# One gate vector of the second layer moves from a row sum to the array, together with changes to banks and instruction order

## The chip, the core and the metric

The kernel runs on one core of a Trainium2 chip. The metric is the device time of one execution in microseconds (us). A core has TensorE (PE), VectorE (DVE), ScalarE (ACT), GpSimd (POOL, unused here) and SyncE (SP), whose queue issues nearly all DMA transfers of this kernel, in program order.

## The reference, cut to what matters

A two-layer transformer step on 384 tokens (one context block of 128 tokens, two latent blocks of 128), 1,024 wide, all in 32-bit floats:

```
mod = silu(cond) @ w_mod[l] + b_mod[l]
sh1, sc1, g1, sh2, sc2, g2 = jnp.split(mod[:, None, :], 6, axis=-1)
u = layer_norm(x) * (1.0 + sc1) + sh1
h = mixer_ab(u, ...) if l == 0 else mixer_cd(u, ...)
x = layer_norm(ALPHA * x + g1 * h, ln_g[l, 0], ln_b[l, 0])
u = layer_norm(x) * (1.0 + sc2) + sh2
x = layer_norm(ALPHA * x + g2 * swiglu(u, w_gate[l], w_up[l], w_down[l]), ln_g[l, 1], ln_b[l, 1])
...
def swiglu(u, w_gate, w_up, w_down):
    return (jax.nn.silu(u @ w_gate) * (u @ w_up)) @ w_down
```

Each layer needs six vectors `mod` of 1,024 numbers, for two conditions (context, latent). Vector (l, v) is the v-th of layer l; (1, 2) is the gate `g1` of layer 1, which is first needed after the second mixer.

## The kernel before, in words

The program goes through layer 0 (mixer AB, output projection, FFN) and layer 1 (mixer CD, output projection, FFN). A 32-bit product is made in three passes (`PASSES`): both operands are split into a rounded part (`r_`, ACT cast, L173) and a rest (`l_`, DVE subtract, L175), and r·r, r·rest and rest·r are summed in PSUM. Weights arrive as pieces of 512 KB in a ring of five buffers `raw` (`raw_unit`), all on SP's queue.

*Modulation vectors* are made in two ways. `mod_pe` multiplies the raw pieces (`rawm`, in the `raw` ring) on the array: 8 pieces, 4 matmuls of 32x256 each. `mod_steps` loads them as `mraw` into the four buffers of the pool `s`, two of which hold the sums `z`. For each of 8 pieces it adds piece times condition to `z` on DVE (L249; the first piece is a multiply on ACT, L246). Then it sums over partitions with 8 matmuls by ones (L254, tile `mod`), scales (`bm`, L258 to L261) and, except for gates, turns the row into columns (`mod_cols`, tile `modc`). A gate's row goes to DRAM (`gs`, 8 small DMAs) and is read back later.

`SMODS` lists the vectors that the two FFNs make with `mod_steps`: six in FFN 0, one in FFN 1. `TMODS` lists those made with `mod_pe` in the transition between the layers, none before. `steps` is called twice for each of ten column groups of an FFN. Before, a call takes up to `MSTEP` pieces, and after a vector's last piece one call is left out.

*Output projection and heads* (`w_out_phase`). For each token block b: projection and residual (`P`), two LayerNorms, then `F` = `to_u`: 8 transposes into two PSUM banks (`puo_b_0`, `puo_b_1`), scaled by ACT or DVE into `ufo`, cast to `urf`, with rest `ulf`. Then `H` = `head`: the first 256 columns of gate and up projection (`hg`, `hu`), their SwiGLU product `hsg`, two transposes (`ht`), and the split `hhr`, `hhl`. `bankTO` hands out two banks, T and O, in turn; `puo` and `ht` share them. The string `WORDER` gives the program order; a scheduler may reorder within an engine, and `boost` raises an operation's priority.

*FFN* (`ffn_phase`): `wg` and `wu` products of 128x384 (L542, two banks of `bankA`), SwiGLU on ACT and DVE (`sg`, `hr`, `hl`), and `dn`, which accumulates the down projection in six banks.

*Transition*: `DORDER` interleaves the last down projections of layer 0 (`D`), LayerNorm (`A`, `B`), transposes (`F`, tiles `pud`, `ufd`, `ur`, `ul`) with `T` = `tail_block`, the first block of the second mixer's slab 1 (`cd_0`). In it `keep_busy` issues `NBUSY` matmuls of 128x512 whose result nobody reads (`idle_d`, L129). `M` = `tail_mod` is defined but not in `DORDER`. After it slab 1 goes on with blocks 1 and 2 (`cd_1`, `cd_2`), then slab 0, 2, 4 and 3. `tck` are transposes of the cached keys `ck`, `tcd` those of a slab's result.

```
for _ in range(MSTEP):
    if next(gen, False):
        st["pause"] = 1
        return
```

Of the kernel before, what the change touches and what calls it, by code (L numbers as in the profile page):

```python
# [19 lines left out]
P = 128  # L20
# [3 lines left out]
NTOK = NB * P  # L24
# [2 lines left out]
HOLD = 4  # L27
RHOLD = (3, 5)
WMODS = ((), ())
TMODS = ()  # L30
SMODS = (((0, 5), (1, 1), (1, 0), (1, 3), (1, 4), (1, 2)), ((1, 5),))
NLNW = 8
AORDER = "Q0 R0 W4 T G0 D V0 M0 Q1 W12 M1 G1 C0 E M2 N1 R1 N2 V1 C1 X N0 N4 N3 N5"
NIDLE = (5, 4)
NFILL = 2
NBUSY = 12
LOADS = (("m", 0, 1), ("kv", 0), ("m", 1, 1), ("q", 0), ("m", 2, 2), ("q", 2), ("m", 4, 2), ("kv", 4), ("q", 4), ("m", 6, 2), ("q", 6))
WORDER = ("P0 P1 G A0 B0 F0 A1 B1 P2 U H0 F1 A2 B2 F2 X H1 M H2", "G P0 P1 A0 B0 A1 B1 U P2 F0 F1 H0 A2 B2 F2 X H1 M H2")
CORDER = "V0 V1 N0 V2 C N1 N2"
DORDER = "D0 A0 D1 B0 A1 F0 U B1 D2 T A2 F1 B2 F2 K"  # L40
NWR = 5
NHEAD = 2
MSTEP = 4
KORDER = ((2, 3, 0, 1), (3, 0, 1, 2))
WDEPTH = 2
RGB = 1
# [18 lines left out]
def trunk_kernel(ctx: ExitStack, tc: tile.TileContext, a: dict):  # L65
    nc = tc.nc
    mm = nc.tensor.matmul
# [169 lines left out]
    def mod_steps(l, v, out):  # L237
        w = a["w_mod"][l].rearrange("(p k) n -> p k n", k=KC)
        bm = mod_tile(l, v)
        z = [big([P, D], f"z{l}_{v}_{c}") for c in range(2)]  # L240
        for k in range(KC):
            t = big([P, D], f"mraw{l}_{v}_{k}")
            SY.dma_start(t, w[:, k, v * D : (v + 1) * D])
            for c in range(2):
                if k == 0:
                    S.mul(z[c], t, cs[:, c, k : k + 1])  # L246
                else:
                    with gated():
# [12 lines left out]
        V.scalar_tensor_tensor(bm, ps[:, 256:512], selc[:, 1:2], bm, ALU.mult, ALU.add)  # L261
        out.append((bm, ps))
# [171 lines left out]
    def w_out_phase(l, pre, cat, x, gt, lnv, u2, sh2, sc2, wx, hh, bankTO, mods):  # L434
# [26 lines left out]
            next(st[b][1])  # L461

        def to_u(b):
            last[b] = make_u(b, st[b][0], sh2, sc2, u2, f"o{l}_{b}", bankTO, b == 2)

        def mod_all():
            for ll, v in mods:
# [2 lines left out]
        def hold_splits():  # L470
            gate[0] = last[2]

        def head(b):
            ps = bankA(f"hg{l}_{b}")
            in_block(ps, u2, units2["g"], b, 256)
            sg = mid([P, 256], f"hsg{l}_{b}")
            S.activation(sg, ps[:, 0:256], AF.Silu)
            ps = bankA(f"hu{l}_{b}")
            in_block(ps, u2, units2["u"], b, 256)
            V.tensor_tensor(sg, ps[:, 0:256], sg, ALU.mult)  # L480
            pt = bankTO(f"ht{l}_{b}")
            for q in range(NHEAD):
                boost(nc.tensor.transpose, pt[:, q * P : (q + 1) * P], sg[:, q * P : (q + 1) * P], ident)
            cat_split(hh, 0, NHEAD, slice(b * P, (b + 1) * P), pt[:, 0 : NHEAD * P])

        run_order(WORDER[l], {"P": project, "A": norm, "B": norm, "F": to_u, "H": head,
                              "G": lambda: head_units("g", a["w_gate"]), "U": lambda: head_units("u", a["w_up"]),
                              "M": mod_all, "X": hold_splits})
        bk.close()


    NF = D_FF // P

    def ffn_phase(l, u2, x, lnp, hh, wx_es, pto, get_g, lnv, steps, keep, late, tail_units, tail_block, tail_mod):
        wg = a["w_gate"][l].rearrange("(k p) f -> p k f", p=P)
        wu = a["w_up"][l].rearrange("(k p) f -> p k f", p=P)
        wd = a["w_down"][l]
# [3 lines left out]
        def load_down(fc, rl=None):  # L501
            return split_unit(wd[fc * P : (fc + 1) * P, :], [D], f"wd{l}_{fc}", rl)

        wx_es.close()
        pto.close()
        fes = ExitStack()
        fpool = fes.enter_context(pool(f"ffn{l}"))
        accp = Banks(f"pd{l}", D=6)
        for fc in range(NHEAD):
# [24 lines left out]
        def proj(w, fp, nm):
            un = [split_unit(w[:, 4 * i : 4 * i + 4, fp * 256 : (fp + 1) * 256], [4, 256], f"{nm}{l}_{fp}_{i}")
                  for i in range(2)]
            ps = [bankA(f"{nm}{l}_{fp}_{j}") for j in range(2)]
            for i in range(2):
                for j in range(2):
                    for k in range(4):  # L540
                        for pu, pw in PASSES:
                            mm(ps[j][:, 0:NTOK], un[i][pw][:, k, j * P : (j + 1) * P], u2[pu][:, 4 * i + k, :],  # L542
                               start=(i == 0 and k == 0 and pu + pw == 0),
                               stop=(i == 1 and k == 3 and pw == 1))
            return ps

        for fp in range(NHEAD // 2, NFP):
            pg = proj(wg, fp, "wg")
            sg = []
            for j in range(2):  # L550
                t = fpool.tile([P, NTOK], F32, tag="sg", name=f"sg{l}_{fp}_{j}", bufs=2)
# [790 lines left out]
    m = {}  # L1342
    xscr = dram.tile([NB, P, D], F32, tag="xscr", name="xscr")
    for l in range(2):
# [31 lines left out]
        u2 = new_u(f"f{l}")  # L1376
        wx, wx_es = opened(f"wx{l}")
        hh = tuple(lnp.tile([P, NHEAD, NTOK], F32R, name=f"hh{q}{l}") for q in "rl")
        w_out_phase(l, pre, cat, x, gt, lnv, u2, m[l, 3], m[l, 4], wx, hh, bankTO, WMODS[l])
        if wxr_es is not None:  # L1380
            wxr_es.close()
        cat_es.close()
# [48 lines left out]
        def steps(fp, i):  # L1431
            if fp == NFP:
                for _ in gen:
                    pass
                at_end()
                return
            if st["pause"]:
                st["pause"] -= 1
                return
            for _ in range(MSTEP):  # L1440
                if next(gen, False):
                    st["pause"] = 1
# [78 lines left out]
```

## Time and profile before

| | |
|---|---|
| Median of three runs | 1017.21 us (1017.24, 1013.7, 1017.21) |
| The profiled execution's own time | 1012.87 us |
| Its span in the trace | 1011.1 us |
| PE busy | 984.2 us, 97% |
| DVE busy | 668.2 us, 66% |
| ACT busy | 436.5 us, 43% |
| DMA read | 167.52 MB, 170 GB/s over the span |

All times in the trace are those of the profiled execution, from the start of its span. Its own time is 1.8 us above the span and 4.3 us below the median. PE's matmuls overlap in the records: an instruction's duration is longer than the distance to the next start, and the distance of starts tells what it costs.

### The profile page before, as it was taken

The numbers are of one execution on the slowest core, as the hardware profiler recorded it, in microseconds if no ns is written. First come the engines' busy times: TensorE is split into PE (matmuls) and PEld (weight loads), VectorE is DVE, ScalarE is ACT, GpSimd is POOL, SyncE is SP. The second block draws the span as 40 slices with busy tenths as digits, with TensorE's granted clock in tenths as the row PEclk, the third lists the DMA queues.
The fourth block names the chain that finished last, engine by engine and source line by source line (L and its number), as shares of the span: only waits on it lengthen the run. The fifth ranks groups of instructions, "written<-read, shape, count | busy, mean of one in ns | idle before, by whom it ended". The sixth has DMA issues, their size and how long they took to land.

```text
span 1011.1 us, 14717 instructions
## 1 busy us (share of the span) xinstructions
PE 984.2 (97%) x5583; PEld 824.0 (81%) x5583; DVE 668.2 (66%) x1368; ACT 436.5 (43%) x790; POOL 1.2 (0%) x5
## 2 busy tenths in 40 slices
PE   9999999999999999999999999999899999999996
PEld 4775567787999888988987766787799999999985
DVE  5387558588875777968978577558895333335554
ACT  3395533228533333334427556544943333333410
POOL 0000000000000000000000000000000000000000
PEclk9999999999999999999999999999999999999999
DMA  9975446473674867768744332235575444444401
GB/s 306 296 205 189 147 140 206 167 252 102 211 229 149 279 203 252 210 219 258 231 168 151 99 95 94 84 106 222 156 237 169 160 123 126 125 124 125 156 22 42
DMA packets 109704, 172.85 MB, mean 171 GB/s; under 512 B 10177, under 2 KB 78273, under 8 KB 109633
## 3 DMA queue, kind: packets, MB, share of 16 engines
q1 hardware_dynamic: 106960, 170.87, 53.0%
q10 hardware_dynamic: 2672, 1.04, 0.4%
q8 instruction: 44, 0.72, 0.3%
q14 instruction: 28, 0.22, 0.1%
HBM read 167.52 MB, written 4.36 MB: 170 GB/s over the span
## 4 chain that ended last, share of the span: by engine, by line
PE 81%; DVE 8%; DMA 4%; ACT 4%; issue 2%; ACTq 0%; DVEq 0%
PE dn L518 17%; PE wg L542 15%; PE wu L542 15%; PE cd L377 7%; PE wo L377 4%; PE rvg L377 3%; PE s L377 3%; DMA rawm<-in_w_mod 2%; PE rqk L377 2%; PE mod L118 2%; DVE z L249 1%; PE ms L118 1%; PE hg L377 1%; PE wpo L118 1%; PE idle L129 1%
## 5 line engine op out<-in xcount | busy, mean ns | idle before, releaser
L249 DVE SCALAR_TENSOR_TENSOR z<-mraw,cs,z 128x1024 f32<-128x1024 f32 x98 | 121.0, 1281 | 12.0 <-DMA mraw<-in_w_mod 11.5
L542 PE MATMUL wg<-urf,r_wg 128*128 128x384 f32 x320 | 108.5, 340 | 3.1 <-DVE sg L559 1.7
L542 PE MATMUL wg<-ulf,r_wg 128*128 128x384 f32 x320 | 108.4, 339 | 0.0
L542 PE MATMUL wu<-ulf,r_wu 128*128 128x384 f32 x320 | 108.2, 338 | 0.0
L542 PE MATMUL wu<-urf,r_wu 128*128 128x384 f32 x320 | 108.2, 340 | 0.0
L542 PE MATMUL wg<-urf,l_wg 128*128 128x384 f32 x320 | 108.1, 338 | 0.0
L542 PE MATMUL wu<-urf,l_wu 128*128 128x384 f32 x320 | 108.1, 338 | 0.0
L175 DVE TENSOR_TENSOR l_wg<-raw_wg,r_wg 128x1024 fp32r<-128x1024 f32 x40 | 48.6, 1224 | 56.2 <-ACT r_wg L173 56.2
L173 ACT CAST r_wd<-raw_wd 128x1024 fp32r<-128x1024 f32 x36 | 37.8, 1049 | 92.0 <-PE wu L542 47.6
L175 DVE TENSOR_TENSOR l_wd<-raw_wd,r_wd 128x1024 fp32r<-128x1024 f32 x36 | 44.0, 1223 | 48.4 <-ACT r_wd L173 48.4
L173 ACT CAST r_wg<-raw_wg 128x1024 fp32r<-128x1024 f32 x40 | 42.0, 1051 | 69.2 <-PE dn L518 32.6
L175 DVE TENSOR_TENSOR l_wu<-raw_wu,r_wu 128x1024 fp32r<-128x1024 f32 x40 | 48.7, 1223 | 33.6 <-ACT r_wu L173 33.6
L518 PE MATMUL dn<-l_wd,hr 128*128 128x512 f32 x168 | 66.6, 396 | 0.0
L518 PE MATMUL dn<-r_wd,hr 128*128 128x512 f32 x168 | 66.6, 396 | 0.0
L518 PE MATMUL dn<-r_wd,hl 128*128 128x512 f32 x168 | 66.5, 396 | 0.0
L542 PEld LDWEIGHTS wg<-urf,r_wg 128*128 128x128 f32 x320 | 60.1, 188 | 6.3 <-DVE sg L559 2.5
L173 ACT CAST r_wu<-raw_wu 128x1024 fp32r<-128x1024 f32 x40 | 42.0, 1049 | 52.9 <-issue 24.7
L542 PEld LDWEIGHTS wu<-urf,r_wu 128*128 128x128 f32 x320 | 60.1, 188 | 2.2 <-ACT r_wg L173 0.8
L542 PEld LDWEIGHTS wu<-ulf,r_wu 128*128 128x128 f32 x320 | 60.1, 188 | 0.5
L542 PEld LDWEIGHTS wg<-ulf,r_wg 128*128 128x128 f32 x320 | 60.1, 188 | 0.4
L542 PEld LDWEIGHTS wg<-urf,l_wg 128*128 128x128 f32 x320 | 60.1, 188 | 0.0
L542 PEld LDWEIGHTS wu<-urf,l_wu 128*128 128x128 f32 x320 | 60.1, 188 | 0.0
(415 smaller groups left out, 2164.2 us busy)
## 6 DMA issues: line engine op xcount, KB each, us to landing
mraw<-in_w_mod SPq DMA_DIRECT2D x56, 512.0 KB
raw_wd<-in_w_down SPq DMA_DIRECT2D x44, 512.0 KB
raw_wg<-in_w_gate SPq DMA_DIRECT2D x40, 512.0 KB
raw_wu<-in_w_up SPq DMA_DIRECT2D x40, 512.0 KB
rawm<-in_w_mod SPq DMA_DIRECT2D x24, 512.0 KB
raw_cd<-in_w_in_cd SPq DMA_DIRECT2D x20, 512.0 KB
ms<-in_w_mod SPq DMA_DIRECT2D x16, 512.0 KB
raw_rqk<-in_w_in_ab SPq DMA_DIRECT2D x16, 256.0 KB
```

The costliest lines, as they stand in the source:

```text
L118: return f(*args, **kw)
L129: mm(ps[0 : lhs.shape[-1], 0 : rhs.shape[-1]], lhs, rhs, start=True, stop=True)
L173: S.copy(r, t)
L175: V.tensor_tensor(lo, t, r, ALU.subtract)
L249: V.scalar_tensor_tensor(z[c], t, cs[:, c, k : k + 1], z[c], ALU.mult, ALU.add)
L377: op = mm(ps[:, col : col + width], u[pu][:, k0 + kk, b * P : (b + 1) * P], (r, lo)[pw][:, kk, :], start=(first and i == 0 and pu + pw == ...
L518: mm(acc[b, nh], h[fc][ph][:, b * P : (b + 1) * P], wrl[pw][:, nh * 512 : (nh + 1) * 512], start=(fc == 0 and ph + pw == 0), stop=(last an ...
L542: mm(ps[j][:, 0:NTOK], un[i][pw][:, k, j * P : (j + 1) * P], u2[pu][:, 4 * i + k, :], start=(i == 0 and k == 0 and pu + pw == 0), stop=(i ...
```

## The change

Vector (1, 2) leaves `SMODS` and enters `TMODS`; `DORDER` runs `M0` right after `T`. The twelve `idle_d` matmuls go (`NBUSY = 0`). `steps` takes two pieces in every call, without a pause: 20 calls of two are the 40 pieces of the five vectors that are left in FFN 0. In `w_out_phase`, `to_u` takes the projection's banks W and V for blocks 1 and 2 and no longer T and O, and the end of a head (`head_end`: `ht`, `hhr`, `hhl`) is written after the next head's gate block, the last one after the FFN's first `wg` projection. The first multiply of a vector is put under `gated()`.

```diff
-TMODS = ()
-SMODS = (((0, 5), (1, 1), (1, 0), (1, 3), (1, 4), (1, 2)), ((1, 5),))
+TMODS = ((1, 2),)
+SMODS = (((0, 5), (1, 1), (1, 0), (1, 3), (1, 4)), ((1, 5),))
-NBUSY = 12
+NBUSY = 0
-DORDER = "D0 A0 D1 B0 A1 F0 U B1 D2 T A2 F1 B2 F2 K"
+DORDER = "D0 A0 D1 B0 A1 F0 U B1 D2 T M0 A2 F1 B2 F2 K"
-MSTEP = 4
+MSTEPS = (2, 2)
...
                 if k == 0:
-                    S.mul(z[c], t, cs[:, c, k : k + 1])
+                    with gated():
+                        S.mul(z[c], t, cs[:, c, k : k + 1])
...
         def to_u(b):
-            last[b] = make_u(b, st[b][0], sh2, sc2, u2, f"o{l}_{b}", bankTO, b == 2)
+            tags = iter((None, "WV", "WW")[b] or ())
+            bank = bankTO if b == 0 else lambda nm: bk(next(tags), nm)
+            last[b] = make_u(b, st[b][0], sh2, sc2, u2, f"o{l}_{b}", bank, b == 2)
...
+        heads = []
+
         def head(b):
             ps = bankA(f"hg{l}_{b}")
             in_block(ps, u2, units2["g"], b, 256)
+            if heads:
+                head_end(*heads.pop())
...
             V.tensor_tensor(sg, ps[:, 0:256], sg, ALU.mult)
+            heads.append((b, sg))
+
+        def head_end(b, sg):
             pt = bankTO(f"ht{l}_{b}")
             for q in range(NHEAD):
-                boost(nc.tensor.transpose, pt[:, q * P : (q + 1) * P], sg[:, q * P : (q + 1) * P], ident)
+                nc.tensor.transpose(pt[:, q * P : (q + 1) * P], sg[:, q * P : (q + 1) * P], ident)
             cat_split(hh, 0, NHEAD, slice(b * P, (b + 1) * P), pt[:, 0 : NHEAD * P])
...
+        return lambda: head_end(*heads.pop())
...
+        first = proj(wg, NHEAD // 2, "wg")
+        end_heads()
+        wx_es.close()
+        pto.close()
...
-            pg = proj(wg, fp, "wg")
+            pg = first if fp == NHEAD // 2 else proj(wg, fp, "wg")
...
-            if st["pause"]:
-                st["pause"] -= 1
-                return
-            for _ in range(MSTEP):
-                if next(gen, False):
-                    st["pause"] = 1
-                    return
-
-        st = {"pause": 0}
+            for _ in range(MSTEPS[i]):
+                next(gen, None)
```

Three places where instructions move. The first is PE in the transition, from the end of slab 1's block 0 (`cd_0`) on. Before:

```order
L377 MATMUL cd_0_5329<-l_cd_3_5263,ur_5051 128x512
L129 MATMUL idle_d<-r_cd_0_5244,ur_5051 128x512 x2
L118 MATMUL pud_0_5384<-ident,sd_1_5141 128x128 x4
L118 MATMUL pud_1_5396<-ident,sd_1_5141 128x128 x4
L129 MATMUL idle_d<-r_cd_0_5244,ur_5051 128x512 x10
L377 MATMUL cd_1_5507<-r_cd_0_5244,ur_5051 128x512
```

PE with the change, at the same place (`tm_2` is the new product, `rawm_2_5` the sixth piece of w_mod):

```order
L378 MATMUL cd_0_5270<-l_cd_3_5204,ur_4992 128x512
L118 MATMUL pud_0_5377<-ident,sd_1_5082 128x128 x4
L118 MATMUL pud_1_5389<-ident,sd_1_5082 128x128 x4
L229 MATMUL tm_2_5298<-rawm_2_0_5304,cmod 32x256 x4
...
L229 MATMUL tm_2_5298<-rawm_2_4_5328,cmod 32x256 x4
L378 MATMUL cd_1_5500<-r_cd_0_5185,ur_4992 128x512
...
L378 MATMUL cd_1_5500<-r_cd_1_5191,ur_4992 128x512
L229 MATMUL tm_2_5298<-rawm_2_5_5334,cmod 32x256
L118 MATMUL pud_0_5411<-ident,sd_2_5217 128x128 x4
L118 MATMUL pud_1_5423<-ident,sd_2_5217 128x128 x4
L229 MATMUL tm_2_5298<-rawm_2_5_5334,cmod 32x256 x3
```

Twenty of the 32 new matmuls stand where ten `idle_d` stood, the other twelve inside `cd_1`, the first of them after seven of its matmuls and ahead of block 2's eight transposes.

The second place is SP's queue in the same stretch. Before, slab 0's four pieces (the `raw_cd` behind slab 1's last one, `raw_cd_3_5260`) are issued around the writes of x to DRAM (`xscr`):

```order
L164 DMA raw_cd_3_5260<-in_w_in_cd 128x2x512
L164 DMA raw_cd_0_5482<-in_w_in_cd 128x2x512
L164 DMA raw_cd_1_5488<-in_w_in_cd 128x2x512
L164 DMA raw_cd_2_5494<-in_w_in_cd 128x2x512
L1389 DMA xscr<-x_0_2368 128x1024
L1389 DMA xscr<-x_1_2369 128x1024
L1326 DMA ct<-in_k_dft 128x2x256
L164 DMA raw_cd_3_5500<-in_w_in_cd 128x2x512
```

SP with the change, from the write of block 2's x on (three `rawm_2` pieces stand ahead of `xscr`, two behind the constants `ct`):

```order
L1402 DMA xscr<-x_2_2370 128x1024
L164 DMA rawm_2_5_5334<-in_w_mod 128x1024
L164 DMA rawm_2_6_5340<-in_w_mod 128x1024
L164 DMA rawm_2_7_5346<-in_w_mod 128x1024
L164 DMA raw_cd_0_5475<-in_w_in_cd 128x2x512
L164 DMA raw_cd_1_5481<-in_w_in_cd 128x2x512
L286 DMA gs_2_5353<-bm_2_5299 1x256 x8
L1181 DMA ck_5461<-in_cache_diff_k 128x512
L1181 DMA ck_5469<-in_cache_diff_k 128x256
L164 DMA raw_cd_2_5487<-in_w_in_cd 128x2x512
L164 DMA raw_cd_3_5493<-in_w_in_cd 128x2x512
```

Slab 0's pieces now stand behind the write of block 2's x, the last three `rawm_2` and, for two of them, behind the eight small writes `gs_2` of the finished vector.

The third place is ACT in layer 0's heads, around the load of the activation table for SiLU. Before:

```order
L246 ACTIVATE z_5_0_3064<-mraw_5_0_3066,cs 128x1024
L477 ACT_TABLE_LOAD
L477 ACTIVATE hsg_0_2725<-hg_0_2700 128x256
L329 ACTIVATE ufo_1_0_2758<-puo_1_0_2759,modc_3_1677,modc_4_1860 128x128 x4
L297 ACTIVATE so_2_2627,lnwbo_2_2793<-x_2_2370,lnwbo_2_2793 128x1024
L391 CAST hhr_2386<-ht_0_2753 128x2x128
L332 CAST urf_2381<-ufo_1_0_2758 128x4x128
L329 ACTIVATE ufo_1_1_2770<-puo_1_1_2771,modc_3_1677,modc_4_1860 128x128 x4
L246 ACTIVATE z_5_1_3065<-mraw_5_0_3066,cs 128x1024
```

ACT with the change:

```order
L247 ACTIVATE z_5_0_3064<-mraw_5_0_3066,cs 128x1024
L247 ACTIVATE z_5_1_3065<-mraw_5_0_3066,cs 128x1024
L484 ACT_TABLE_LOAD
L484 ACTIVATE hsg_0_2725<-hg_0_2700 128x256
L330 ACTIVATE ufo_1_0_2753<-puo_1_0_2754,modc_3_1677,modc_4_1860 128x128 x4
L330 ACTIVATE ufo_1_1_2765<-puo_1_1_2766,modc_3_1677,modc_4_1860 128x128
L333 CAST urf_2381<-ufo_1_0_2753 128x4x128
L330 ACTIVATE ufo_1_1_2765<-puo_1_1_2766,modc_3_1677,modc_4_1860 128x128 x3
L298 ACTIVATE so_2_2627,lnwbo_2_2788<-x_2_2370,lnwbo_2_2788 128x1024
L333 CAST urf_2381<-ufo_1_1_2765 128x4x128
L392 CAST hhr_2386<-ht_0_2850 128x2x128
```

Block 1's four `ufo_1_1` and the multiply `z_5_1` now stand ahead of the statistics of block 2 (`so_2`, L297 before, L298 with the change).

## Rows read from the trace of the kernel before

**Rows 1.** the page's busy times (busy us, share, instructions), and its chain that ended last

```profile
PE 984.2 (97%) x5583; PEld 824.0 (81%) x5583; DVE 668.2 (66%) x1368; ACT 436.5 (43%) x790; POOL 1.2 (0%) x5
...
PE 81%; DVE 8%; DMA 4%; ACT 4%; issue 2%; ACTq 0%; DVEq 0%
```

**Rows 2.** timeline of PE, layer 0 heads: start, us, instruction, [idle before <-releaser]

```profile
253.22 0.66 PE L118 MATMUL puo<-ident,so 128*128 128x128 f32 x4 [1.18 <-DVE hhl L392]
...
255.52 1.09 PE L118 MATMUL puo<-ident,so 128*128 128x128 f32 x8
...
260.57 0.28 PE L377 MATMUL hg<-r_gh,urf 128*128 128x256 f32 x1
```

**Rows 3.** timeline of ACT, layer 0 heads

```profile
251.14 1.17 ACT L297 ACTIVATE so<-x,lnwbo 128x1024 f32<-128x1024 f32 x1
...
255.30 1.16 ACT L246 ACTIVATE z<-mraw,cs 128x1024 f32<-128x1024 f32 x1
...
256.85 1.52 ACT L329 ACTIVATE ufo<-puo,modc,modc 128x128 f32<-128x128 f32 x4
258.53 0.62 ACT L332 CAST urf<-ufo 128x512 fp32r<-128x512 f32 x1 [0.15 <-DVE ufo L326]
```

**Rows 4.** busy by stretch: start:end, length, PE, PEld, DVE, ACT, POOL, granted clock, DMA share, GB/s

```profile
243.00:269.00 26.00, 23.27 (x181) 21.98 (x180) 22.07 (x55) 21.36 (x39) 0.00 (x0) 1.00 0.51 159
269.00:531.00 262.00, 258.92 (x1415) 236.74 (x1414) 205.28 (x237) 92.38 (x113) 0.00 (x0) 1.00 0.69 221
480.00:500.00 20.00, 19.64 (x107) 18.85 (x107) 19.31 (x18) 8.23 (x11) 0.00 (x0) 1.00 0.82 266
1000.00:1011.00 11.00, 2.18 (x10) 1.42 (x8) 5.47 (x18) 1.24 (x2) 0.00 (x0) 0.81 0.13 48
```

**Rows 5.** groups of instructions: count | busy us, mean ns | idle before, releasers

```profile
L249 DVE SCALAR_TENSOR_TENSOR z<-mraw,cs,z 128x1024 f32<-128x1024 f32 x98 | 121.0, 1281 | 12.0 <-DMA mraw<-in_w_mod 11.5
L542 PE MATMUL wg<-urf,r_wg 128*128 128x384 f32 x320 | 108.5, 340 | 3.1 <-DVE sg L559 1.7 <-ACT sg L552 0.7 <-DVE modc L272 0.6
```

**Rows 6.** chain of waits, end of FFN 0: start, us, what

```profile
469.83 3.70 PE wu L542 x21
473.53 1.05 PE mod L254 x16
...
474.59 5.39 DMA mraw<-in_w_mod
...
484.79 1.22 DVE l_wg L175
...
487.06 2.48 DVE z L249 x2
...
499.28 0.48 DVE hl L566
```

**Rows 7.** timeline of PE, transition

```profile
548.96 2.57 PE L129 MATMUL idle_d<-r_cd,ur 128*128 128x512 f32 x10
552.34 0.50 PE L377 MATMUL cd<-r_cd,ur 128*128 128x512 f32 x1 [0.81 <-ACT ur L332]
...
556.89 0.39 PE L377 MATMUL cd<-r_cd,ur 128*128 128x512 f32 x1
...
559.45 0.39 PE L377 MATMUL cd<-l_cd,ur 128*128 128x512 f32 x1
```

**Rows 8.** timeline of SP's queue, transition

```profile
508.49 4.28 SPq L285 DMA_DIRECT2D gs<-bm  x8
...
549.96 0.34 SPq L1389 DMA_DIRECT2D xscr<-x  x1
```

**Rows 9.** chain of waits, pieces rawm of an earlier vector

```profile
164.73 3.66 DMA rawm<-in_w_mod
...
175.94 5.58 DMA rawm<-in_w_mod
```

**Rows 10.** timeline of PE, layer 1 heads

```profile
725.39 0.39 PE L377 MATMUL hg<-r_gh,urf 128*128 128x256 f32 x1 [1.32 <-ACT hsg L477]
```

More of the change, by code (lines that the diff above doesn't have):

```diff
@@ L489, in w_out_phase, with ffn_phase @@
         bk.close()
+        return lambda: head_end(*heads.pop())
     NF = D_FF // P
-    def ffn_phase(l, u2, x, lnp, hh, wx_es, pto, get_g, lnv, steps, keep, late, tail_units, tail_block, tail_mod):
+    def ffn_phase(l, u2, x, lnp, hh, wx_es, pto, get_g, lnv, steps, keep, late, tail_units, tail_block, tail_mod, end_heads):
         wg = a["w_gate"][l].rearrange("(k p) f -> p k f", p=P)
@@ L502, in load_down, with proj @@
             return split_unit(wd[fc * P : (fc + 1) * P, :], [D], f"wd{l}_{fc}", rl)
+        fes = ExitStack()
+        def proj(w, fp, nm):
+            un = [split_unit(w[:, 4 * i : 4 * i + 4, fp * 256 : (fp + 1) * 256], [4, 256], f"{nm}{l}_{fp}_{i}")
+                  for i in range(2)]
+            ps = [bankA(f"{nm}{l}_{fp}_{j}") for j in range(2)]
+            for i in range(2):
+                for j in range(2):
+                    for k in range(4):
+                        for pu, pw in PASSES:
+                            mm(ps[j][:, 0:NTOK], un[i][pw][:, k, j * P : (j + 1) * P], u2[pu][:, 4 * i + k, :],
+                               start=(i == 0 and k == 0 and pu + pw == 0),
+                               stop=(i == 1 and k == 3 and pw == 1))
+            return ps
+        first = proj(wg, NHEAD // 2, "wg")
+        end_heads()
         wx_es.close()
         pto.close()
-        fes = ExitStack()
         fpool = fes.enter_context(pool(f"ffn{l}"))
@@ L532, in stream_down @@
                     down(fc, wrl, b, nh)
[L534 to L545, printed above, removed]
         for fp in range(NHEAD // 2, NFP):
-            pg = proj(wg, fp, "wg")
+            pg = first if fp == NHEAD // 2 else proj(wg, fp, "wg")
             sg = []
@@ L1378, in trunk_kernel @@
         hh = tuple(lnp.tile([P, NHEAD, NTOK], F32R, name=f"hh{q}{l}") for q in "rl")
-        w_out_phase(l, pre, cat, x, gt, lnv, u2, m[l, 3], m[l, 4], wx, hh, bankTO, WMODS[l])
+        end_heads = w_out_phase(l, pre, cat, x, gt, lnv, u2, m[l, 3], m[l, 4], wx, hh, bankTO, WMODS[l])
         if wxr_es is not None:
@@ L1436, in steps @@
                 return
-            if st["pause"]:
-                st["pause"] -= 1
-                return
-            for _ in range(MSTEP):
-                if next(gen, False):
-                    st["pause"] = 1
-                    return
-        st = {"pause": 0}
+            for _ in range(MSTEPS[i]):
+                next(gen, None)
         ffn_phase(l, u2, x, lnp, hh, wx_es, pto, lambda: load_g(lnp, m[l, 5], f"g2_{l}"), lnv2, steps, keep, late,
-                  tail_units, tail_block, tail_mod)
+                  tail_units, tail_block, tail_mod, end_heads)
         les.close()
```

## The prediction

> **What bounds the kernel now.** I read the page first: PE is busy for 97% of the span, and 81% of the chain that ended last is PE [rows 1]. So nothing that shortens DVE, ACT or DMA counts unless PE waits for it, and every matmul that is added counts unless it lies in such a wait. The second view is PE's timeline, for its idle time. It lies in few places: the heads of layer 0, where PE is busy for 23.27 of 26 us; FFN 0, where it is busy for 258.92 of 262 [rows 4]; the transition between the layers; and the heads of layer 1. The third view, the groups of instructions, names FFN 0's waits: 3.1 us in all, 1.7 of them for the SwiGLU product on DVE, 0.7 for SiLU on ACT and 0.6 for a vector's columns [rows 5]. DVE is nearly full when this happens: 19.31 of 20 us from 480 to 500, at 266 GB/s, while over the whole FFN it is busy for 205 of 262 us at 221 GB/s [rows 4]. The waits come from bursts of four pieces, not from DVE's total. The fourth view, the timelines of ACT and SP, shows what is late in the heads and the transition.
>
> **Heads of layer 0.** Two things change. The second half of block 1's transposes (`puo_1_1`) no longer shares a bank with `ht_0`, so PE's wait of 1.18 us for the split of `ht_0` on DVE [rows 2] goes. On the other side ACT's order changes: `z_5_1` (1.16 us) and the four `ufo_1_1` (1.50 us, as the four at 256.85 show) now stand ahead of the statistics of block 2, which started at 251.14 [rows 3]. They come 1.16 + 1.50 = 2.66 us later, and block 2's transposes, at 255.52 before [rows 2], come at 258.2. ACT then has less left to do: before, block 2's first `ufo` started at 256.85, behind `z_5_1` at 255.30 [rows 3]; now it starts as soon as the first four transposes are through, about half of the 1.09 us of all eight [rows 2] later, at 258.7. That is 1.85 us later. Block 2's first `urf` ended at 258.53 + 0.62 = 259.15 [rows 3] and now ends at 261.0. Before, PE began `hg_2` at 260.57, which was 1.4 us after that [rows 2]; half of this I take as slack, since the rest part `ulf` has to be made as well. So `hg_2` starts at 261.7: **+1.1 us**. Bounds: -1.2 if only the bank's wait counts, +2.7 if the whole delay does. That `ht` comes later costs nothing; it is needed only by the first `dn`.
>
> **FFN 0.** One vector of six goes. On DVE that is 14 `z` operations of 1.24 us [rows 6], 17.4 us, none of which PE waits for except through the burst waits. On PE it is the 8 matmuls by ones: 1.05 us [rows 6], all on the path, as PE does not pause elsewhere here. With two pieces in each call DVE gets about 5 us of `z` per half column group, with no run of four pieces beside a full load stream; I take the three waits as gone, **-3.1** [rows 5], and **-1.05** for the matmuls.
>
> But without the pauses and with exactly 40 pieces in 20 calls, the last vector (tile `mod_4`) ends with the FFN. PE has 48 `wu_9`, 48 `wg_10` and 48 `wu_10` between the ones-matmuls of the fourth vector and those of the fifth; at 3.70 us for 21 [rows 6] these 144 take 25.4, and with a few short matmuls 26.0 us. The fifth vector's second piece can only be loaded when the fourth's `z` buffers are free, thus behind its ones-matmuls. DVE's side of the same stretch: 5.39 us for that load, as at 474.59; 14 `z` of 1.24, 17.4; two splits of 1.22; five SwiGLU steps of 0.48 [rows 6]. Sum 5.39 + 17.4 + 2.44 + 2.4 = 27.6. So PE waits at the end for 27.6 - 26.0 = **+1.6 us**. Bounds: nothing, if the load takes 3.66, which a piece of this size took elsewhere [rows 9]; 3.3, if each of the seven pieces is late by the mean of before: 12.0 us of DVE's idle time ahead of 98 `z` [rows 5], 0.245 per operation, 1.7 for seven pairs at one wait each. FFN 0 in sum: -3.1 - 1.05 + 1.6 = **-2.55**, between -4.15 and, if the three waits stay, +2.25.
>
> **Transition.** The 32 new matmuls have the shape of the ones-matmuls in their output (32x256), so 1.05 / 8 = 0.131 us each [rows 6], 4.2 us in all. Twenty lie where ten `idle_d` ended and PE then waited 0.81 us for `ur` until 552.34 [rows 7]: from 548.96 on they take 2.6 of 3.4 us. They are free, and so is the removal of `idle_d`, because the wait for `ur`, not the fillers, ends last there. The other twelve are on the path: **+1.6**. The first of them needs the sixth piece. That load stands on SP behind the write of block 2's x, which was issued at 549.96 and took 0.34 [rows 8], so it goes out at 550.3; at the mean of 3.66 and 5.58, the shortest and longest landing of a row of such pieces [rows 9], it lands at 554.9. PE gets there after seven matmuls of `cd_1`, spaced (559.45 - 556.89) / 11 = 0.233 [rows 7]: 552.34 + 1.63 = 554.0. It waits **+0.9**. Behind this matmul block 2's transposes queue up on PE, and ACT waits for them; they stood at a similar time before, so nothing more is late. Slab 0's last two pieces now go out behind eight small writes (4.28 us for eight [rows 8]) that wait for the finished vector. After 554.9 that takes twelve new matmuls (1.6), eight transposes (1.0) and seven of `cd_1` (1.6), so until 559.1; the two pieces go out near 563.9 and land near 568.5. PE has ten more matmuls of `cd_1`, 24 of `cd_2` (7.9 us) and a dozen small transposes (some 1.5) before slab 0's block 0, which starts near 568.5 and needs the third piece 12 matmuls, 2.8 us, later: covered, with about 1.5 us to spare after the split of 1.22 [rows 6]. Transition: **+2.5**, between +1.6 and, with 5.58 for the landing, +3.5.
>
> Here a rule of the Trainium skill speaks against the change: the page TensorE: Matmul & The Clock Gate, in the section Why this matters for your kernels, advises against idle gaps of TensorE between bursts of matmuls, since an array that idles falls from 2.4 to 1.2 GHz. By that the removed fillers would have had a use, and the forecast would rise by the half clock priced among the rivals. The trace agrees that the clock falls at all: in the last 11 us PE works for 2.18, and the granted clock is 0.81 [rows 4]. But FFN 0 has a wait of 1.7 us [rows 5], and its granted clock is 1.00 throughout [rows 4]. The wait that I expect, 0.9 us, is shorter.
>
> **Layer 1 and the rest.** The heads there keep ACT's order up to `hsg_0`, for which PE waits 1.32 us [rows 10]: 0, or -1.3 if the banks free it. FFN 1 makes the same single vector, and `gated()` holds an instruction back on DVE, while the multiply is ACT's: 0.
>
> **The sum.** +1.1 - 2.55 + 2.5 = **+1.05 us**. The profiled execution took 1012.87 us and would take 1013.9; the median shown is 1017.21, 4.3 us above it with nothing changed, and becomes **1018.3**. That spread of the runs is also why I take 0.5%, 5.1 us, as about what can be told from no change.
>
> **Rivals.**
> - *All waits go*: the idle 2.73 us of layer 0's heads (26 - 23.27 [rows 4]), FFN 0 at -4.15, layer 1's 1.32 [rows 10], transition +1.6. Sum -6.6: 1010.6. For it: PE was the only full engine. Against it: block 2's chain on ACT is later in the order. Chance 0.20.
> - *The transition starves*: the last three pieces land one behind the other, not together. Each then takes 4.6 us (the mean of 3.66 and 5.58 [rows 9]), the last lands at 550.3 + 13.8 = 564.1 and not by the 558.6 at which PE wants it, +5.5 more: 1023.8, and slab 0's pieces slip with it. It decides from the moment the eighth piece lands after 558.6. For it: SP issues them in one queue. Against it: their buffers come free together. Chance 0.13.
> - *The even spread does nothing*, as the waits come from the transfers and not from the bursts: the 3.1 stay, 1021.4. Against it: DVE's 19.31 of 20 us. Chance 0.12.
> - *The clock falls* in the transition: the remaining 17 matmuls of `cd_1`, 17 x 0.233 = 4.0 us, take twice as long: 1022.3. Chance 0.03.
>
> **How the numbers follow.** My forecast has 0.52, with its own range from 1014.5 to 1021.5 by the bounds of single terms. Faster by over 0.5% is the first rival: 0.20. Slower by over 0.5% (above 1022.3) is the second, with a part of the fourth: 0.14. The rest is 0.66. The range reaches into the first two rivals, 1011.5 to 1022.5, and leaves out about half of the first and of the second.
>
> **What would show it.** In the heads, no wait of PE for `hhl` at `puo_1_1`, and `hg_2` waiting for `urf` or `ulf` up to 1 us later than 260.57. In FFN 0, no waits of `wg` for `sg` or `modc` in the bursts' places, DVE busy near 70% throughout, and a wait of PE ahead of `mod_4` that ends with `z`. In the transition, `tm_2` at about 549 with no idle time, a wait for `rawm` near 554, and `cd_0` of slab 0 about 2.5 us later against its block before. A granted clock under 1.00 there, a second wait for `rawm`, or a wait for `raw_cd` at slab 0 would prove me wrong, and so would heads that end earlier than before.

## The result and the profile after

The changed kernel takes 1021.15 us (median of 11 runs, 1018.23 to 1028.58) against 1014.4 us of the kernel before (11 runs, 1009.93 to 1017.24). The ratio is 1.0075, 95% interval [1.0055, 1.0094]: slower by 5.6 to 9.5 us. The profiled execution took 1019.96 us, 7.1 more than that of before. The forecast of 1018.3 erred by 3 us and its range holds the result, but by luck: it started from the median of three runs, 1017.21, which is 2.8 us above that of eleven. The change itself was forecast at +1.05 us, at most +5.3, and came out at about +7.6. The case that I gave 0.66, no change within 0.5%, did not come; slower by over 0.5%, which I gave 0.14, did.

The page's busy times and its chain, which answer to [rows 1]:

```profile
PE 987.7 (97%) x5619; PEld 824.7 (81%) x5619; DVE 651.2 (64%) x1353; ACT 434.5 (43%) x788; POOL 1.2 (0%) x5
...
PE 82%; DVE 6%; DMA 5%; ACT 5%; issue 2%; SPq 0%; ACTq 0%; DVEq 0%
```

DVE has 17 us less to do, as planned, and PE is busy for 3.5 us more. To see where the 7 us are, I compare when PE begins the same work in both profiles: the first `hg`, `wg`, `cd` and `td` (transposes of the first attention probabilities, behind slab 1, blocks 0 and 1 of slab 0 and the first matmul of its block 2).

| | first hg | first wg | first cd | first td | heads (hg to wg) | FFN 0 (wg to cd) | transition (cd to td) |
|---|---|---|---|---|---|---|---|
| before | 243.35 | 266.61 | 542.11 | 579.66 | 23.26 | 275.50 | 37.55 |
| changed | 244.22 | 270.55 | 543.22 | 587.06 | 26.33 | 272.67 | 43.84 |
| difference | 0.87 | | | | +3.07 | -2.83 | **+6.29** |

The 0.87 us ahead of `hg` lie in identical code, and are within the spread there: the first `hg` stands between 243.18 and 248.18 us in the profiles of this document. The transition loses 6.3 us, the heads 3.1, and FFN 0 gives 2.8 back. PE's timeline in the transition (answers to [rows 7]):

```profile
549.78 2.37 PE L229 MATMUL tm<-rawm,cmod 128*32 128x256 f32 x40
553.03 0.50 PE L378 MATMUL cd<-r_cd,ur 128*128 128x512 f32 x1 [0.88 <-ACT ur L333]
553.95 0.50 PE L378 MATMUL cd<-r_cd,ul 128*128 128x512 f32 x1 [0.42 <-DVE ul L334]
...
556.17 0.62 PE L229 MATMUL tm<-rawm,cmod 128*32 128x256 f32 x2 [0.55 <-DMA rawm<-in_w_mod]
...
564.72 0.50 PE L378 MATMUL cd<-r_cd,ur 128*128 128x512 f32 x1 [0.22 <-ACT dkT L387]
...
569.23 0.60 PE L118 MATMUL tck<-ident,ck 128*128 128x128 f32 x4
...
571.41 0.44 PE L118 MATMUL tcd<-ident,t1cd 128*128 128x128 f32 x2 [0.20 <-DVE t1cd L407]
572.66 0.44 PE L118 MATMUL tcd<-ident,t1cd 128*128 128x128 f32 x2 [0.82 <-ACT dqT L387]
574.07 0.47 PE L378 MATMUL cd<-r_cd,ur 128*128 128x512 f32 x1 [0.97 <-DVE t2cd L406]
```

The first twenty `tm` (40 records) end under the wait for `ur`, of which 0.88 us is left: free, as forecast. The sixth piece is late and PE waits 0.55 us. `cd_1` runs from 553.03 to `cd_2` at 564.72, 11.7 us, and `cd_2` to slab 0 at 574.07, 9.35 us. Before, `cd_1` ran from 552.34 [rows 7] to 559.93, 7.6 us, and `cd_2` to 566.74, 6.8:

```profile
559.93 0.50 PE L377 MATMUL cd<-r_cd,ur 128*128 128x512 f32 x1
...
566.74 0.40 PE L377 MATMUL cd<-r_cd,ur 128*128 128x512 f32 x1
```

In `cd_2` lie three waits, of 0.20, 0.82 and 0.97 us near 572, that I had not expected. SP's queue in the same stretch (answers to [rows 8]):

```profile
550.05 0.38 SPq L1402 DMA_DIRECT2D xscr<-x  x1
550.53 1.77 SPq L164 DMA_DIRECT2D rawm<-in_w_mod  x3
552.40 1.92 SPq L164 DMA_DIRECT2D raw_cd<-in_w_in_cd  x2
561.81 2.31 SPq L286 DMA_DIRECT2D gs<-bm  x8
564.22 0.84 SPq L1181 DMA_DIRECT2D ck<-in_cache_diff_k  x2
565.15 8.84 SPq L164 DMA_DIRECT2D raw_cd<-in_w_in_cd  x6
```

Nothing goes out on SP from 554.3 to 561.8, where the queue waits for the vector `bm`. The cached keys `ck` leave at 564.2, before at 556.85:

```profile
556.85 2.79 SPq L1168 DMA_DIRECT2D ck<-in_cache_diff_k  x2
```

The chain of waits names what ends last in the changed kernel's stretch:

```profile
549.86 0.67 PE tm L229 x9
550.53 5.60 DMA rawm<-in_w_mod
556.17 0.62 PE tm L229 x2
...
557.81 0.56 PE tm L229 x6
...
558.80 0.57 PE tm L229 x8
...
560.72 0.57 PE tm L229 x8
...
571.02 0.37 ACT dkT L387
571.39 0.95 ACT r_cd L173
572.40 1.11 issue
573.51 0.43 DVE t2cd L406
573.94 0.14 issue
574.07 2.10 PE cd L378 x8
```

The twelve `tm` inside `cd_1` (24 records) take 0.62 + 0.56 + 0.57 + 0.57 = 2.3 us of the chain, not 1.6. The waits near 572 are for copies (`dkT`, `dqT`) and steps of the rotary embedding (`t1cd`, `t2cd`), which ACT and DVE make between splits of slab 0.

The heads, on PE (answers to [rows 2]) and by the stretch's clock (start:end, length, PE, PEld, DVE, ACT, POOL, granted clock, DMA share, GB/s):

```profile
252.88 0.44 PE L493 MATMUL ht<-ident,hsg 128*128 128x128 f32 x2 [0.57 <-DVE hsg L487]
254.08 0.39 PE L378 MATMUL hg<-r_gh,urf 128*128 128x256 f32 x1 [0.76 <-ACT urf L333]
254.81 0.39 PE L378 MATMUL hg<-r_gh,ulf 128*128 128x256 f32 x1 [0.23 <-DVE ulf L334]
263.91 0.38 PE L378 MATMUL hg<-r_gh,urf 128*128 128x256 f32 x1 [0.98 <-ACT urf L333]
264.63 0.39 PE L378 MATMUL hg<-r_gh,ulf 128*128 128x256 f32 x1 [0.34 <-DVE ulf L334]
```

```profile
250.00:260.00 10.00, 8.44 (x55) 7.79 (x54) 5.42 (x19) 6.97 (x16) 0.00 (x0) 0.83 0.50 157
```

The wait for `hhl` is gone, and `hg_2` (263.91) waits for `urf`, as forecast. But in place of the 1.18 us for `hhl` [rows 2] `hg_1` now waits 0.76 and 0.23 us for its own `urf` and `ulf`, so that the new bank gives little back. New is the clock: 0.83 in the mean from 250 to 260, behind waits of 0.57, 0.76 and 0.23 us. FFN 0 keeps three waits, 1.6 us together, at other places; the last two are those for the last vector's sums:

```profile
484.33 0.45 PE L524 MATMUL wu<-urf,r_wu 128*128 128x384 f32 x1 [0.42 <-ACT sg L565]
...
511.08 0.64 PE L255 MATMUL mod<-z,ones 128*32 128x256 f32 x8 [0.63 <-DVE sg L572]
512.27 0.64 PE L255 MATMUL mod<-z,ones 128*32 128x256 f32 x8 [0.55 <-DVE z L250]
```

### The profile page after: what moved, and what is told of

Same layout as the page of the kernel before. It is cut to its first block, busy times and chain, and to the rows that moved or that the text cites. A ratio compares the mean times of both kernels' runs of the same rounds, so it can differ in the third digit from the quotient of the medians.

```text
span 1018.1 us, 14767 instructions
## 1 busy us (share of the span) xinstructions
PE 987.7 (97%) x5619; PEld 824.7 (81%) x5619; DVE 651.2 (64%) x1353; ACT 434.5 (43%) x788; POOL 1.2 (0%) x5
## 4 chain that ended last, share of the span: by engine, by line
PE 82%; DVE 6%; DMA 5%; ACT 5%; issue 2%; SPq 0%; ACTq 0%; DVEq 0%
PE dn L544 17%; PE wg L524 16%; PE wu L524 15%; PE cd L378 7%; PE wo L378 4%; PE rvg L378 3%; DMA rawm<-in_w_mod 3%; PE s L378 2%; PE rqk L378 2%; PE mod L118 1%; DMA mraw<-in_w_mod 1%; PE hg L378 1%; PE ms L118 1%; ACT ufo L330 1%; DVE z L250 1%
## 5 line engine op out<-in xcount | busy, mean ns | idle before, releaser
L250 DVE SCALAR_TENSOR_TENSOR z<-mraw,cs,z 128x1024 f32<-128x1024 f32 x84 | 104.4, 1280 | 7.3 <-DMA mraw<-in_w_mod 7.1
```

## The experiments

Theory A says that the transition's late loads are most of the loss, with the heads' order on ACT second. Its rivals were the missing fillers, the new matmuls as such, and FFN 0. All ratios are to the kernel before, run on the same chip. The three stretches are those of the table above, from each run's profile; a star marks one in which the granted clock fell (a mean of 0.83 or less over 10 us).

| run | ratio, 95% interval | heads | FFN 0 | transition |
|---|---|---|---|---|
| changed kernel | 1.0075 [1.0055, 1.0094] | 26.33* | 272.67 | 43.84 |
| x1: no vector | 1.0024 [1.0011, 1.0037] | 26.35* | 273.10 | 39.84* |
| x2: no small writes | 1.0047 [1.0031, 1.0062] | 24.85 | 273.77 | 41.41 |
| x3: old heads | 1.0052 [1.0036, 1.0067] | 23.29 | 274.56 | 43.96 |
| x5: five pieces | 1.0021 [1.0006, 1.0036] | 24.85 | 276.20* | 38.52 |
| x4: even six | 1.0008 [0.9996, 1.0020] | 24.51* | 276.16* | 38.06 |
| x8: before, no fillers | 1.0022 [1.0007, 1.0037] | 23.28 | 275.79 | 39.93* |
| x6: banks only | 1.0086 [1.0070, 1.0102] | 26.19* | 275.75* | 43.59 |
| x9: no vector, fillers | 1.0039 [1.0023, 1.0054] | 24.84 | 275.18* | 37.55 |
| y1: vector only | 1.0032 [1.0018, 1.0047] | 23.27 | 273.42 | 43.88 |
| y2: heads only | 1.0012 [0.9997, 1.0027] | 26.33* | 275.41 | 37.53 |
| y4: FFN 0 only | 1.0004 [0.9988, 1.0020] | 23.26 | 273.53 | 37.50 |
| y3: mended | 1.0020 [1.0004, 1.0036] | 24.47* | 273.41 | 41.47 |

Where the clock held, two of the stretches repeat closely: the old heads take 23.26 to 23.29 us in five profiles, and the transition with the vector and its writes on SP 43.59 to 43.96 in four. FFN 0 with five vectors does not: 272.67 to 274.56 in seven.

**x1, the changed kernel without the vector.**

```diff
-TMODS = ((1, 2),)
+TMODS = ()
...
                     m[ll, v] = mod_scratch(out[0][0], nm)
+                    if (ll, v) == (0, 5):
+                        m[1, 2] = m[0, 5]
```

> The changed kernel without the vector (1, 2): it is made neither in rows nor on the array, and layer 1 reads FFN 0's gate in its place (so the output differs). Heads, banks, steps and the missing fillers stay as changed; slab 0's loads return to their old place in the queue. In the two profiles, from block 1's transposes in the transition (532.42 before, 533.54 after) to the same transpose in slab 4 (597.54 and 604.96) the change loses 6.3 us; the heads up to hg_2 lose 2.5, FFN 0 wins 2.2. Theory A (the new work and its loads in the transition are the loss): that stretch is as long as before within 0.5 us, also without fillers, and the time is within 2 us of the kernel before, some 6 us under the changed one. Theory B (the loss is the missing fillers or the order of the heads): the stretch stays at least 3 us longer than before, or the time stays at least 4 us above the kernel before.

The time falls from 1.0075 to 1.0024. The transition is 39.84 us, 4.0 under the changed kernel and still 2.3 above before; those 2.3 are the clock, below. Neither of A's two marks is met (about 2.3 us for 0.5 in the stretch, 2.4 for 2 in the time), nor either of B's (3 and 4 us). The vector and what comes with it in the transition are the greater part of the loss.

**x2, the vector made but not written to DRAM**, with the gate aliased as in x1.

```diff
-                    mod_now(ll, v, bankA(f"tm{ll}_{v}"))
+                    mod_pe(ll, v, bankA(f"tm{ll}_{v}"), mm)
```

> The changed kernel, but the finished vector is not written to DRAM (the eight small writes gs are left out and layer 1 reads FFN 0's gate, so the output differs). All 32 matmuls and 8 loads stay. Theory A1 (slab 0's last two pieces are late because they stand behind the eight writes, which wait for the vector; their splits then push the copies and the RoPE of slab 1's last blocks back): the pieces go out 2 to 4 us earlier, PE's three waits of 0.20, 0.82 and 0.97 us before slab 0 go, and the time falls by 2 us, to about 4 to 5 us above the kernel before. Theory A2 (they are late for want of ring buffers, which the matmuls free): the waits stay and the time changes by under 0.5 us.

The transition loses 2.4 us less (41.41) and the time falls to 1.0047. SP goes on earlier:

```profile
551.83 1.11 SPq L164 DMA_DIRECT2D raw_cd<-in_w_in_cd  x2
560.13 0.34 SPq L1181 DMA_DIRECT2D ck<-in_cache_diff_k  x1
560.58 0.37 SPq L164 DMA_DIRECT2D raw_cd<-in_w_in_cd  x1
```

Even without the writes the queue stands from 552.9 to 560.1, for another wait, which the profile puts down to `ul` on DVE. Measured from the first `cd`, the writes hold the keys back by 3.5 us and not by the whole 7.5. PE's transposes are no longer crowded at the end of `cd_2`, and of the three waits near 572 none is left:

```profile
564.32 0.50 PE L378 MATMUL cd<-r_cd,ur 128*128 128x512 f32 x1 [0.22 <-ACT dkT L387]
564.66 0.60 PE L118 MATMUL tck<-ident,ck 128*128 128x128 f32 x4
566.72 0.38 PE L118 MATMUL tck<-ident,ck 128*128 128x128 f32 x2
566.93 0.38 PE L118 MATMUL tcd<-ident,t1cd 128*128 128x128 f32 x2
567.86 0.44 PE L118 MATMUL tcd<-ident,t1cd 128*128 128x128 f32 x2
...
571.17 0.39 PE L378 MATMUL cd<-r_cd,ur 128*128 128x512 f32 x1
```

In the changed kernel `tck` came behind 19 matmuls of `cd_2`, here behind one, and slab 1's last transposes `tcd` followed close behind it. `cd_2` takes 6.85 us, from 564.32 to slab 0 at 571.17, as before the change (6.81), while `cd_1` stays at 11.85. So the writes cost what `cd_2` lost, 2.5 us, and nothing of `cd_1`; A1 had about the right size. Which of the two held up `cd_2`, the late keys or slab 0's late pieces, this run does not separate, since both go out earlier and the scheduler places `tck` earlier too.

**x5, five pieces loaded.**

```diff
+            if (l, v) == (1, 2) and k >= 5:
+                t = held[k - 3]
```

> The changed kernel, but only five of the vector's eight pieces are loaded; the last three products read pieces 2 to 4 again (so the output differs). The 32 matmuls stay and now all stand ahead of cd_1, under the wait for ur; no load of the vector is issued behind the write of x, and the eight small writes go out earlier. Theory A (late pieces cost most: the wait at the sixth, the matmuls scattered among cd_1, slab 0's loads behind them): 32 x 0.131 = 4.2 us against about 3.3 us of cover, so about 1 us is lost in the transition in place of 6.3, and the time is about 5 us under the changed kernel, 1 to 2 above the kernel before. Rival (the matmuls themselves cost it): the transition still loses at least 4 us.

The transition takes 38.52 us, 1.0 above before, with all 32 matmuls in it. They stand in one row under the wait for `ur`:

```profile
550.79 3.66 PE L234 MATMUL tm<-rawm,cmod 128*32 128x256 f32 x64
```

So the matmuls (3.66 us for 32) are not the cost. What costs is that three of eight pieces come after the wait is over: the wait for them, the scattered matmuls, and the writes and loads that queue up behind. x5 takes these away together; only the writes are tested by themselves (x2). x5's time, 1.0021, is 5.5 us under the changed kernel's.

**x8, the kernel before without fillers.**

```diff
-NBUSY = 12
+NBUSY = 0
```

> The kernel before with one edit: no idle_d matmuls. Theory A (the wait for ur ends last whether PE fills it or not): the transition is as long as before, PE idles for about 3.3 us ahead of cd_1, the time is within 0.5 us of the kernel before. Rival (an idle PE loses its clock): the granted clock is 0.5 for some microseconds behind that idle time, as at 553 to 560 in the run without the vector, and the time is 1 to 2 us above the kernel before, with a mean clock of the runs lower by 0.002 or more.

The rival held, at the upper end of its size. One edit that removes twelve matmuls whose result nobody reads makes the kernel slower by 0.7 to 3.7 us. PE's timeline and the clock of the 10 us around it:

```profile
549.10 1.09 PE L118 MATMUL pud<-ident,sd 128*128 128x128 f32 x8 [0.18 <-ACT sd L312]
...
553.34 0.80 PE L377 MATMUL cd<-r_cd,ur 128*128 128x512 f32 x1 [3.14 <-ACT ur L332]
```

```profile
550.00:560.00 10.00, 6.86 (x26) 5.41 (x24) 3.71 (x16) 6.87 (x16) 0.00 (x0) 0.66 0.37 120
```

PE idles for 3.14 us, and the first `cd_1` matmul behind it takes 0.80 us, before 0.50 [rows 7]. The transition is 2.4 us longer than before, and the mean clock of the ten runs is 0.9946, that of before 0.9966 (25 runs).

**x9, x1 with the twelve fillers back.**

```diff
-NBUSY = 0
+NBUSY = 12
```

> The changed kernel without the vector (1, 2), as in the first run, but with the twelve idle_d matmuls back; layer 1 reads FFN 0's gate, so the output differs. The first run stood at 1.0024 of the kernel before, with a granted clock of 0.5 from 553 to 559 behind 3.15 us of idle PE. Theory of the clock: the transition no longer loses its clock, the runs' mean clock rises by 0.001 to 0.003, and the time falls by 0.7 to 1.7 us. Rival (the fillers are hidden and do nothing): no change of the time.

The profile says yes: the transition is 37.55 us, to the digit that of before, and the runs' mean clock is 0.9962, in x1 0.9942. The time says no: 1.0039 against x1's 1.0024, with intervals that overlap, on another chip. For the time it stays undecided; x8 is the clearer test. The three stretches of x9 are together 1.3 us longer than before and the time 3.9; this gap is open.

**x3, the old heads in the changed kernel.** The edit takes the change's part in `to_u` and `head` back, and the FFN starts behind the last head:

```diff
-            last[b] = make_u(b, st[b][0], sh2, sc2, u2, f"o{l}_{b}", bank, b == 2)
+            last[b] = make_u(b, st[b][0], sh2, sc2, u2, f"o{l}_{b}", bankTO, b == 2)
...
-            heads.append((b, sg))
...
+                boost(nc.tensor.transpose, pt[:, q * P : (q + 1) * P], sg[:, q * P : (q + 1) * P], ident)
```

> The changed kernel with the heads of the kernel before: banks T and O for all transposes, ht directly behind its head, boosted. The rest as changed. Theory A (block 2's statistics are late on ACT behind z_5_1 and ufo_1_1): hg_2 starts 2 to 2.5 us earlier against the first hg_0, and the time falls by 2 to 2.5 us, to about 4 to 5 us above the kernel before. Rival (what the heads lose was waiting anyway and is taken back in the FFN): the time stays as changed, 6 to 7 us above.

1.0052: by the middle values the heads' part costs 2.3 us of the 7.6, though the two intervals overlap. The heads take 23.29 us again.

**x6, the new banks with the old place of ht.** As x3, without its first two lines:

```diff
-            heads.append((b, sg))
...
+                boost(nc.tensor.transpose, pt[:, q * P : (q + 1) * P], sg[:, q * P : (q + 1) * P], ident)
```

> The changed kernel with the heads' transposes in the banks W and V as changed, but ht boosted and directly behind its head, and the FFN begun after it, as before. z_5_1 and ufo_1_1 still stand ahead of block 2's statistics on ACT. Theory A (that order on ACT is what the heads lose): the heads lose as in the changed kernel, hg_2 waits for urf, and the time is 6 to 8 us above the kernel before. Rival (the deferral of ht loses it): as with the old heads, some 5 us above.

1.0086, 8.7 us and so a little more than expected: the deferral of `ht` is not what loses. ACT keeps `z_5_1` and `ufo_1_1` ahead of block 2's statistics, and the heads take 26.19 us, with the clock down as in the changed kernel.

**y1, the title's change alone**, in the kernel before.

```diff
-TMODS = ()
+TMODS = ((1, 2),)
-SMODS = (((0, 5), (1, 1), (1, 0), (1, 3), (1, 4), (1, 2)), ((1, 5),))
+SMODS = (((0, 5), (1, 1), (1, 0), (1, 3), (1, 4)), ((1, 5),))
...
-NBUSY = 12
+NBUSY = 0
...
-DORDER = "D0 A0 D1 B0 A1 F0 U B1 D2 T A2 F1 B2 F2 K"
+DORDER = "D0 A0 D1 B0 A1 F0 U B1 D2 T M0 A2 F1 B2 F2 K"
```

> The kernel before with the title's change alone: vector (1, 2) goes from FFN 0 to the transition and its 32 matmuls take the place of the twelve idle_d. Bursts of four with a pause in FFN 0 and the heads as before. By the earlier runs the move costs the transition 5 to 6 us (changed kernel 1.0075, without the vector 1.0024, with pieces in time 1.0021, without the small writes 1.0047); FFN 0 gives back 1.05 us of ones-matmuls and perhaps one burst's wait. Theory A (the transition is most of the loss): 4 to 6 us above the kernel before. Rival (the loss needs the heads' new order or the even steps as well): under 2 us above.

1.0032, a little under what was expected. The transition takes 43.88 us, the same as in the changed kernel, and FFN 0 gives 2.1 back.

**y2, the heads' part alone**: the changed kernel with the constants and the steps of before.

```diff
-TMODS = ((1, 2),)
+TMODS = ()
...
-NBUSY = 0
+NBUSY = 12
...
-MSTEPS = (2, 2)
+MSTEP = 4
```

> The kernel before with the heads' part of the change alone: banks W and V, ht deferred, the FFN's first wg projection ahead of the last head's end. Vectors, bursts, fillers and transition as before. Theory A (z_5_1 and ufo_1_1 ahead of block 2's statistics make hg_2 wait, and the idle time lets the clock fall for some 3 us in most executions): the heads are 1.5 us longer, 3 us where the clock falls, and the time is 1.5 to 3 us above the kernel before. Rival (only together with the even steps): within 1 us of it.

1.0012 [0.9997, 1.0027]: in the time not told from no change, and so not decided; in the profile the heads are 3.07 us longer, as in the changed kernel. The heads' part is thus 1.2 us by this run, 2.3 by x3 and 2.7 by y3 against x2.

**y4, FFN 0's part alone**, in the kernel before, with the gate aliased as in x1.

```diff
-SMODS = (((0, 5), (1, 1), (1, 0), (1, 3), (1, 4), (1, 2)), ((1, 5),))
+SMODS = (((0, 5), (1, 1), (1, 0), (1, 3), (1, 4)), ((1, 5),))
...
-MSTEP = 4
+MSTEPS = (2, 2)
...
```

> The kernel before with FFN 0's part of the change alone: five vectors, two pieces in each call. Vector (1, 2) is left out altogether and layer 1 reads FFN 0's gate (so the output differs); heads, fillers and transition as before. Theory A (the bursts' 3.1 us of waits go, 1.05 of matmuls go, 1.5 to 2.5 of waits for the last vector's sums come): 1.5 to 3 us under the kernel before. Rival (the waits only move, and DVE's end lets the clock fall at 510 us, as it did in three of the profiles): within 1 us of it.

FFN 0 is 2.0 us shorter in the profile, but the time does not show it (1.0004), so the rival held. The waits are moved, not gone, 2.0 us together for 3.1 before [rows 5]:

```profile
483.92 0.45 PE L542 MATMUL wu<-urf,r_wu 128*128 128x384 f32 x1 [0.35 <-ACT sg L552]
...
488.66 0.42 PE L542 MATMUL wu<-urf,r_wu 128*128 128x384 f32 x1 [0.51 <-DVE modc L272]
...
511.28 0.64 PE L254 MATMUL mod<-z,ones 128*32 128x256 f32 x8 [0.56 <-DVE sg L559]
512.47 0.64 PE L254 MATMUL mod<-z,ones 128*32 128x256 f32 x8 [0.55 <-DVE z L249]
```

y1, with five vectors in bursts, has a FFN 0 as short as this (273.42 against 273.53). The vector less is the gain; the even steps are none. In three of the ten profiles with five vectors (x5, x6, x9) the clock fell behind the waits near 511, to a mean of 0.83 from 510 to 520, and FFN 0 took 275.2 to 276.2 us, for 275.5 before: of the gain at most 0.3 us was left. How often that happens in executions without a profile is not shown.

**x4, six vectors in even steps**, in the kernel before.

```diff
-MSTEP = 4
+MSTEPS = (3, 2)
```

> The kernel before with one edit: all six vectors stay in FFN 0, but their 48 pieces are taken evenly, three and two by turns, and not in bursts of four with a pause. Heads, transition and fillers as before. Theory A (the 3.1 us of waits in FFN 0 come from the bursts): they go, and a wait for the last z at the end of the FFN of up to 2 us comes; the time is 1 to 3 us under the kernel before. Rival (the waits come from DVE's and the transfers' total in these stretches): they come back elsewhere in the FFN, and the time is within 1 us of the kernel before. The changed kernel's FFN 0 with the old heads, from hg to the first pud, is 0.9 us shorter than before with a vector less, which speaks for the rival.

1.0008: the rival held, and even steps alone win nothing. Of 3.1 us of waits in FFN 0 2.4 are left, 1.91 of them one wait for SiLU on ACT, behind which the clock fell in this profile.

**y3, old heads and the small writes on GpSimd's queue.**

```diff
-                SY.dma_start(sc[cnd, j : j + 1, :], mp[32 * j + cnd : 32 * j + cnd + 1, :])
+                (G if name == "1_2" else SY).dma_start(sc[cnd, j : j + 1, :], mp[32 * j + cnd : 32 * j + cnd + 1, :])
```

> The changed kernel with two of its losses mended: the old heads, and the eight small writes of vector (1, 2) issued on GpSimd's queue, which is empty, so that SP's queue goes on to the cached keys and slab 0's last pieces. If the two add up (2.3 us for the heads, 2.8 for the writes, from the earlier runs): 2 to 3 us above the kernel before. If the pieces' lateness returns in another place: 5 us above, as with the old heads alone.

1.0020: 5.6 us of the loss are gone, and the two mends add up (2.3 and 2.8). The transition takes 41.47 us, as in x2. No version beat the kernel before. A mend of the rest would need all eight pieces in place when the wait for `ur` begins, with a ring of five buffers; it was not tried.

## Why the prediction was right in part and wrong in part

**Transition: forecast +2.5, measured +6.3.** This is the step that failed. The 6.3 us are -0.4 in `cd_0`, +4.1 in `cd_1`, +2.5 in `cd_2` and +0.1 from there to `td`. Right was that twenty of the matmuls are free, and that the sixth piece is late (wait 0.55 us, forecast 0.9). Three things were missed. First, the price of the other twelve, 0.131 each from a row of eight back to back; scattered among `cd_1` they took 2.3 us for 1.6. Second, "nothing more is late" behind the sixth piece: `cd_1` is 4.1 us longer where 2.5 was forecast. The twelve matmuls make 2.3 of it and the waits of 0.42 (for `ul`, which two transposes `tcd` had partly covered before), 0.55 and 0.22 us another 1.2; some 0.6 is not resolved. Third, "covered, with about 1.5 us to spare" for slab 0: this counted when pieces land, and not what is queued in order behind the eight writes, on SP the keys, on PE `tck` and both `tcd`, on ACT and DVE the splits between the copies. That is the +2.5 of `cd_2`: without the writes on SP it takes 6.85 us (x2) and 6.86 (y3), with them 9.35. The same three in the title's change alone (y1) cost the same.

**The clock: rated 0.03 for the transition.** There it held at 1.00, so the rival as stated did not come; but "The wait that I expect, 0.9 us, is shorter" was the wrong comparison, twice. The fillers did serve: without them and without other work in their place (x8), the clock falls and 2.4 us of the transition go with it. In the changed kernel the twenty `tm` took their place. And elsewhere the clock fell behind several short waits: in the changed kernel's heads behind 0.57, 0.76 and 0.23 us of idle time within 2.5 us. It did not always: x2, x5 and x9 have the same waits at 1.00, and what decides stays open. The Trainium skill (TensorE: Matmul & The Clock Gate, section Why this matters for your kernels), which I set aside, advises to leave no idle gaps between bursts of matmuls; for x8's 3.14 us the trace agrees.

**Heads: forecast +1.1, bounds -1.2 to +2.7.** Without the fall of the clock they take 24.85 us (x2, x5), +1.6, by the mechanism named: `hg_2` waits for `urf` behind late statistics, and against the first `hg` it starts 1.0 us later in x2. In four of seven profiles with ACT's new order the clock fell too, another 1.5 us; of seven with the old order it fell in two, for 1.2. That term was not in the forecast.

**FFN 0: forecast -2.55, measured -2.8 in the changed kernel, -2.0 (y4) and -2.1 (y1).** The size is about right where the clock held (-0.9 to -2.8 in seven profiles); where it fell (three) it was -0.3 to +0.7. Two of the parts are wrong. The 3.1 us of waits do not come from the bursts, since x4 keeps six vectors, spreads them evenly and still waits 2.4 us. The wait of 1.6 us for the last vector did come, as 0.63 + 0.55 in the changed kernel.

**Layer 1 and `gated()`: forecast 0.** The heads of layer 1 take 23.57 us, before 23.78, and FFN 1 is the same to 0.1 us.

**Sum.** +1.6 with 1.5 for the clock, -2.8 and +6.3 make 6.6, beside 0.87 that the two profiles differ by ahead of all changes; the measured 7.6 has an interval of 5.6 to 9.5. That the range of the forecast holds the time owes to its base: with the median of eleven runs, 1014.4, in place of 1017.21 the same bounds would end at 1019.7. The rival "the transition starves" was the nearest to what happened, by another path: not the pieces one behind the other, but an in-order queue that holds up what stands behind them.

## What to carry to other kernels

When work moves into a wait, ask whether its last input is there before the wait is over; what comes later sits in the open, and so does everything that in-order queues hold behind it, down to transfers that have nothing to do with it. Small writes of a result belong on a queue where nothing urgent follows (x2, y3). Filler matmuls in a wait can keep up the clock behind it, as they do here (x8): take them out only where other work of PE takes their place. And forecast the change, not the time: a base of three runs was 2.8 us off here.

## What the runs showed of the hardware that I had not expected

The granted clock fell behind 3.14 us of idle PE (x8: a mean of 0.66 from 550 to 560, and 0.50, which is 1.2 GHz, from 553 to 559). In some executions it fell behind several waits of under 1 us each (0.83 from 250 to 260 in the changed kernel's heads, and 0.50 from 256 to 258); in others with the same heads it did not. The time goes with it: mean clocks of single runs of the kernel before go from 0.994 to 0.998, and of the 35 runs beside y1 those at 0.994 took 1017.7 us in the mean, those at 0.998 1012.8.
